# An MLP up-projection with seven block products in place of eight, in four token quarters, and score and value matmuls in alternating order

## The chip, the core and the metric

The kernel runs on one core of one Trainium2 chip. The core has a matrix engine (TensorE, PE in the profile, with PEld for its weight loads), a vector engine (VectorE, DVE), a scalar engine (ScalarE, ACT), a general engine (GpSimd, POOL) and a queue that issues transfers (SyncE, SP). Each engine takes its instructions in the order in which the program lists them. Matmul results go to PSUM, everything else lives in SBUF. The metric is the device time of one execution in microseconds.

## The reference

One inference step of a one-layer decoder: 2048 prompt tokens and 32 sample tokens (8 sequences of 4) of width 1024. Cut to what matters:

```python
p = einsum('btd,de->bte', h, w_in)                 # input projection
s = einsum('bnqgrd,bnkgd->bngrqk', qb, kk)         # scores of a 128-token window, head dim 64
o = einsum('bngrqk,bnkgd->bnqgrd', softmax(s), vv) # values
mixed = einsum('bte,ed->btd', concatenate([y_ssm, o], -1), w_out)
x = layer_norm(ALPHA * x + g_m * mixed)
h = x * (1.0 + sc_f) + sh_f
u = square(relu(einsum('btd,df->btf', h, w_up)))   # 1024 -> 4096
f = einsum('btf,fd->btd', u, w_down)               # 4096 -> 1024
x = layer_norm(ALPHA * x + g_f * f)
```

All inputs and outputs are float32. The kernel forms nearly every large product in three matmuls on rounded halves: each operand is split into a high part and a remainder (`hi` and `lo`), and `hi*hi + hi*lo + lo*hi` is accumulated in PSUM.

## The kernel before

The program has four stages: the first sweep over 17 token tiles (input projection of dt, q, k, v and the windowed attention), a second sweep (the state-space branch), the output projection with its LayerNorm, and the MLP. A scheduler that works on estimated durations lays out the order of each engine from the order of the calls, so an edit can move instructions that it doesn't touch.

In the first sweep `st_score` forms the scores of a tile with 24 matmuls `sc<-kTh,qh` (lines 166 to 168) whose contraction is 64 rows; four heads sit in rows 0 to 63 and four in rows 64 to 127 of the array, and the code issues all of one half's matmuls of a group before the other's. `st_PV` (line 462) issues the two 64-column halves of the value product in turn.

In the MLP the 2048 prompt tokens go in two halves of 1024. For each of 32 blocks of 128 hidden columns, `up` multiplies the block's weights (8 blocks of 128 rows) with the half's activations `H`, in groups of 512 columns (first half) or of 352 (second half, which takes the 32 sample tokens along): 8 x 3 matmuls a group. ScalarE takes relu and square, VectorE squares again in full precision (line 1269) and GpSimd forms the remainder (line 1270). `down` then takes two blocks at a time: 8 token tiles x 2 column halves x 2 blocks x 3 matmuls of 512 columns; VectorE adds each result from PSUM to an SBUF accumulator (line 1299). The weights come from HBM once a half. An up block is split by ScalarE (hi, line 162) and GpSimd (lo, line 163); a down block is first multiplied by the gate row `gf` on VectorE (line 1137). At the half's end the accumulators are normalised and stored (`finish`), and during each half the residual is added (lines 1230 to 1232).

## Time and profile before

| | us |
|---|---|
| three runs | 2469.86, 2470.47, 2472.53 (median 2470.47) |
| profiled execution | 2467.04, its span 2465.2 |
| MLP stage in the trace (first up matmul to last down matmul) | 978 to 2446 |
| output projection | 792 to 978 |
| first sweep's attention | 66 to 400 |

A row of the trace gives the start or the busy time, the engine, the line and the tiles `out<-in`. Busy times of one engine can't be added to another's, since the engines run side by side; an engine's busy time also holds the time in which an instruction has started and can't get on.

### The profile page before, as it was taken

How to read it: one execution, taken by the hardware profiler on the slowest of the kernel's cores; microseconds unless marked ns; L12 is line 12 of the kernel's file. 1: busy time of each engine (PE TensorE's matmuls, PEld its weight loads, DVE VectorE, ACT ScalarE, POOL GpSimd, SP SyncE). 2: the span in 40 equal slices, each digit the busy share in tenths (PEclk: the TensorE clock that was granted, in tenths of full speed). 3: DMA queues.
4: the chain of work that ended last, by engine and by line, in shares of the span. 5: the costliest groups of instructions: out<-in, count | busy, mean ns of one | idle time of the engine just before them, and what ended most of it. 6: DMA issues, size and time to landing. Idle time of an engine off the chain costs nothing.

```text
span 2465.2 us, 32266 instructions
## 1 busy us (share of the span) xinstructions
PE 2401.8 (97%) x12695; PEld 1997.0 (81%) x12695; DVE 1458.2 (59%) x2533; ACT 783.7 (32%) x1578; POOL 857.9 (35%) x587
## 2 busy tenths in 40 slices
PE   7899999999999999999999999999999999999997
PEld 6567777987897888887888888888889889889885
DVE  6756565987789776356555444448354554453448
ACT  3544455432333545421211212213412212212221
POOL 4333341233223222532332424327333333323335
PEclk9999999999999999999999999999999999999998
DMA  8754242223315346322121211118211211111111
GB/s 315 255 189 167 81 166 70 88 63 121 101 37 198 134 153 218 123 76 70 56 69 52 73 43 52 52 35 218 76 60 43 67 54 52 52 51 35 46 45 71
DMA packets 116104, 242.11 MB, mean 98 GB/s; under 512 B 26080, under 2 KB 61360, under 8 KB 112800
## 3 DMA queue, kind: packets, MB, share of 16 engines
q1 hardware_dynamic: 111552, 230.07, 27.9%
q10 hardware_dynamic: 4400, 9.98, 1.1%
q8 instruction: 100, 1.64, 0.3%
q14 instruction: 52, 0.43, 0.1%
HBM read 185.66 MB, written 55.37 MB: 98 GB/s over the span
## 4 chain that ended last, share of the span: by engine, by line
PE 49%; DVE 2%; POOL 1%; issue 1%; ACT 0%; DMA 0%; POOLq 0%; DVEq 0%; ACTq 0%
PE sc L166 10%; PE sc L168 10%; PE sc L167 10%; PE mm L166 5%; PE mm L168 5%; PE mm L167 5%; PE tr L166 1%; PE tr L168 1%; PE tr L167 1%; PE tr L1284 1%; DVE p L1299 1%; DVE nb L1311 0%; DVE p L1318 0%; POOL rs L174 0%; DVE bst L1332 0%
## 5 line engine op out<-in xcount | busy, mean ns | idle before, releaser
L163 POOL TENSOR_TENSOR wdl<-st,wdh 128x1024 fp32r<-128x1024 f32 x63 | 153.7, 2440 | 480.6 <-ACT wdh L162 480.6
L1269 DVE TENSOR_TENSOR r<-r 128x320 f32<-128x320 f32 (+1 forms) x160 | 131.1, 821 | 300.0 <-ACT A L1265 102.4
L1299 DVE TENSOR_TENSOR p<-mm,p 128x512 f32<-128x512 f32 x278 | 187.7, 685 | 123.2 <-PE mm L168 123.0
L162 ACT ACTIVATE wdh<-st 128x1024 fp32r<-128x1024 f32 x63 | 66.9, 1061 | 558.7 <-PE mm L168 173.0
L166 PE MATMUL sc<-H,wvh 128*128 128x352 f32 (+1 forms) x640 | 225.6, 352 | 5.0 <-ACT r L1263 5.0
L167 PE MATMUL sc<-H,wvh 128*128 128x352 f32 (+1 forms) x640 | 225.8, 353 | 0.0
L168 PE MATMUL sc<-H,wvl 128*128 128x352 f32 (+1 forms) x640 | 225.6, 352 | 0.0
L166 PE MATMUL sc<-H,wuh 128*128 128x352 f32 (+1 forms) x640 | 223.8, 350 | 0.0
L168 PE MATMUL sc<-H,wul 128*128 128x352 f32 (+1 forms) x640 | 223.1, 349 | 0.0
L167 PE MATMUL sc<-H,wuh 128*128 128x352 f32 (+1 forms) x640 | 222.9, 348 | 0.0
L1263 ACT ACTIVATE r<-sc 128x352 f32<-128x352 f32 (+1 forms) x160 | 81.6, 511 | 292.1 <-PE sc L168 281.9
L1137 DVE TENSOR_TENSOR st<-st,gf 128x1024 f32<-128x1024 f32 x64 | 112.6, 1759 | 95.4 <-POOL wdl L163 65.5
L166 PEld LDWEIGHTS sc<-H,wvh 128*128 128x128 f32 x640 | 120.6, 189 | 17.8 <-ACT r L1263 5.4
L167 PEld LDWEIGHTS sc<-H,wvh 128*128 128x128 f32 x640 | 120.6, 188 | 12.3
L168 PEld LDWEIGHTS sc<-H,wvl 128*128 128x128 f32 x640 | 120.5, 188 | 11.9
L166 PEld LDWEIGHTS sc<-H,wuh 128*128 128x128 f32 x640 | 120.1, 188 | 11.1 <-ACT r L1263 0.8
L168 PEld LDWEIGHTS sc<-H,wul 128*128 128x128 f32 x640 | 120.5, 188 | 10.2
L167 PEld LDWEIGHTS sc<-H,wuh 128*128 128x128 f32 x640 | 120.3, 188 | 10.0
L174 POOL TENSOR_TENSOR rs<-ve,mhalf 128x1 f32<-128x1 f32 (+2 forms) x68 | 48.5, 713 | 204.6 <-DVE ve L173 187.8
L653 DVE SCALAR_TENSOR_TENSOR xc<-xq,cvw,xc 128x256 f32<-128x256 f32 x192 | 102.2, 536 | 2.7
L1268 DVE TENSOR_TENSOR ud<-r 128x32 f32<-128x32 f32 x32 | 48.2, 1506 | 91.1 <-ACT r L1263 91.1
L163 POOL TENSOR_TENSOR wvl<-st,wvh 128x1024 fp32r<-128x1024 f32 x32 | 77.1, 2411 | 63.7 <-ACT wvh L162 60.7
(489 smaller groups left out, 6567.3 us busy)
## 6 DMA issues: line engine op xcount, KB each, us to landing
st<-in_wd SPq DMA_DIRECT2D x64, 512.0 KB
st<-in_wu SPq DMA_DIRECT2D x63, 512.0 KB
wa<-in_w_ada SPq DMA_DIRECT2D x32, 512.0 KB
hT_d<-hb SPq DMA_DIRECT2D x16, 1024.0 KB
hT<-hT_d SPq DMA_DIRECT2D x16, 512.0 KB
hT<-hT_d SPq DMA_DIRECT2D x8, 1024.0 KB
csb<-cs_d SPq DMA_DIRECT2D x16, 512.0 KB
st<-xhat_d SPq DMA_DIRECT2D x16, 512.0 KB
```

Of the source, the lines that this page charges most:

```text
L162: S.activation(hi, src, AF.Copy)
L163: (eng or V).tensor_tensor(lo, src, hi.bitcast(F32), ALU.subtract)
L166: PE.matmul(out, lhsT=ahi, rhs=bhi, start=first, stop=False)
L167: PE.matmul(out, lhsT=ahi, rhs=blo, start=False, stop=False)
L168: PE.matmul(out, lhsT=alo, rhs=bhi, start=False, stop=last)
L174: G.tensor_tensor(r[:P], v[:P], mhalf[:P, 0:n], ALU.pow)
L653: V.scalar_tensor_tensor(dst_, src(j), cvw[:, f, j:j + 1], dst_, ALU.mult, ALU.add)
L1137: V.tensor_tensor(st, raw, scale, ALU.mult)
L1263: S.activation(r[:, :n], mm[:, :n], AF.Relu)
L1268: V.tensor_tensor(ud, r[:, w:n], r[:, w:n], ALU.mult)
L1269: V.tensor_tensor(r[:, :w], r[:, :w], r[:, :w], ALU.mult)
L1299: V.tensor_tensor(acc[t][:, sl], mm, acc[t][:, sl], ALU.add)
```

## The change

Two edits. In the first sweep, the score matmuls of the two halves of the array are now issued in turn (rows 64 to 127, rows 0 to 63, and so on), tied into that order by `side_by_side`; each group of two heads gets a PSUM bank of its own, and the first is tied behind a projection matmul (`mid`). The value matmuls are tied in turn in the same way. On TensorE, one tile's scores, before and now (kTh, kTl, qh, ql: high and low parts of keys and queries; sc and mm are PSUM banks):

```order
L166 MATMUL sc<-kTh,qh 128x256
L167 MATMUL sc<-kTl,qh 128x256
L168 MATMUL sc<-kTh,ql 128x256
L166 MATMUL sc<-kTh,qh 128x256
L167 MATMUL sc<-kTl,qh 128x256
L168 MATMUL sc<-kTh,ql 128x256
```

```order
L440 MATMUL mm<-kTl,qh 128x256
L440 MATMUL sc<-kTl,qh 128x256
L440 MATMUL mm<-kTh,ql 128x256
L440 MATMUL sc<-kTh,ql 128x256
L440 MATMUL mm<-kTh,qh 128x256
L440 MATMUL sc<-kTh,qh 128x256
```

What moved: the three products of one head came one after another, and now the same product of two heads in different rows stands side by side.

In the MLP, the tokens go in four quarters of 512 (the last with the 32 sample tokens), and one step takes a pair of hidden blocks (256 columns). The product of a 2 x 2 block matrix of weights (hidden block by half of the 1024 rows) with a 2 x 2 block matrix of activations (half of the rows by even or odd token tile) is formed from seven products of sums of blocks instead of eight products. Each product has 4 x 3 matmuls of 256 columns (272 in the last quarter). The sums of activation blocks (`h_ops`) are formed once a quarter, those of weight blocks (`up_ops`) once for each pair in each quarter, and the results are put together from PSUM by seven VectorE additions and one ScalarE copy a step. Both weight matrices are now loaded, scaled and split four times instead of twice. ScalarE's relu and square become one VectorE instruction on each hidden block (line 1339).

One turn of VectorE's work in the MLP, before (one turn is two hidden blocks and 1024 tokens; r: relu; st<-st,gf: scaled down weights; p: accumulators; mm and tr: PSUM banks):

```order
L1137 TENSOR_TENSOR st_13033<-st,gf 128x1024
L1269 TENSOR_TENSOR r<-r 128x512
L1137 TENSOR_TENSOR st_13041<-st,gf 128x1024
L1269 TENSOR_TENSOR r<-r 128x512 x2
L1299 TENSOR_TENSOR p_10009<-tr,p_10009 128x512
L1269 TENSOR_TENSOR r<-r 128x512
L1299 TENSOR_TENSOR p_10009<-mm,p_10009 128x512
L1299 TENSOR_TENSOR p_10010<-mm,p_10010 128x512 x2
L1299 TENSOR_TENSOR p_10011<-tr,p_10011 128x512 x2
```

and the first part of one now (two hidden blocks and 512 tokens; ws, wra, wrc, w1l, wBl: sums of weight blocks and their remainders; U, c: sums of products, sc: the products in PSUM; ho holds the gate row):

```order
L1175 TENSOR_TENSOR ws<-wrc 128x512
L1177 TENSOR_TENSOR wrc<-wra,wrc 128x512
L1325 TENSOR_TENSOR U_14189<-sc,X_14188 128x256
L1255 TENSOR_TENSOR st_14549<-p_14545,ho 128x1024
L1325 TENSOR_TENSOR c_14191<-sc,X_14188 128x256
L1325 TENSOR_TENSOR c_14191<-sc,U_14189 128x256
L1172 TENSOR_TENSOR w1l<-ws,w1h 128x512
L1325 TENSOR_TENSOR U_14190<-sc,U_14189 128x256
L1178 TENSOR_TENSOR wra<-ws,wra 128x512
L1325 TENSOR_TENSOR c_14192<-sc,U_14190 128x256
L1374 TENSOR_TENSOR p_13898<-tr,p_13898 128x512
L1179 TENSOR_TENSOR wra<-wra 128x512
```

What moved: the additions that free PSUM stood in rows of their own, and now stand one by one between additions whose inputs are both in SBUF.

GpSimd's order, one step now (u and B: remainders of the hidden values; wCl, wAl: of weight sums; wdl: of down weights); before, the same four weight splits and four remainders served twice the tokens:

```order
L172 TENSOR_TENSOR wdl<-st_16521,wdh 128x1024
L1345 TENSOR_TENSOR B_16272<-c_16170,A_16271 128x512
L1172 TENSOR_TENSOR wCl<-wrc,wCh 128x1024
L1345 TENSOR_TENSOR B_16272<-c_16171,A_16271 128x512
L172 TENSOR_TENSOR wdl<-st_16529,wdh 128x1024
L1172 TENSOR_TENSOR wAl<-wra,wAh 128x1024
```

What moved: nothing stands between the four weight splits of a step but the two remainders.

The diff, cut to its core:

```diff
+    def side_by_side(calls, prev=None):
+        for fn in calls:
+            ins = fn()
+            if prev is not None:
+                tc.add_manual_dep(ins.ins, prev.ins.name,
+                                  mybir.DependencyInfo(mybir.DependencyClass.NoSync, mybir.DependencyReason.DATA),
+                                  reason="side_by_side")
+            prev = ins
...
+        mid = tl.pop("mid", None)
+        rp = lambda par: slice(64 * par, 64 * par + 64)
         for g in range(2):
+            scs = [(sc_tile, mm_tile)[g * par]().rearrange("p (j s n) -> p j s n", j=2, s=2) for par in range(2)]
+            side_by_side([lambda jj=jj, i=i, par=par: PE.matmul(
+                scs[par][:, jj, 0:nk, :], lhsT=(ql if i == 2 else qh)[rp(par), 2 * g + jj, :],
+                rhs=(kTl if i == 1 else kTh)[rp(par), g, slots, :], start=i == 0, stop=i == 2)
+                for jj in range(2) for i in range(3) for par in (1, 0)], mid)
             for par in range(2):
-                sc = sc_tile().rearrange("p (j s n) -> p j s n", j=2, s=2)
-                rp = slice(64 * par, 64 * par + 64)
-                for jj in range(2):
-                    q2 = 2 * g + jj
-                    mm3(sc[:, jj, 0:nk, :], qh[rp, q2, :], ql[rp, q2, :], kTh[rp, g, slots, :], kTl[rp, g, slots, :])
+                sc = scs[par]
...
-        for i, (vv, pt) in enumerate(terms):
-            for g in range(2):
-                PE.matmul(o[64 * g:64 * g + 64, :], lhsT=vv[:, 64 * g:64 * g + 64], rhs=pt[:, g, :],
-                          start=i == 0, stop=i == len(terms) - 1, tile_position=(0, 64 * g))
+        side_by_side([lambda i=i, vv=vv, pt=pt, g=g: PE.matmul(
+            o[64 * g:64 * g + 64, :], lhsT=vv[:, 64 * g:64 * g + 64], rhs=pt[:, g, :], start=i == 0,
+            stop=i == len(terms) - 1, tile_position=(0, 64 * g))
+            for i, (vv, pt) in enumerate(terms) for g in (1, 0)])
...
+    def h_ops(e, o, sl):
+        b11, b21, b12, b22 = e[:, 0:4], e[:, 4:8], o[:, 0:4], o[:, 4:8]
+
+        def put(i, t):
+            S.activation(HH[i][:, :, sl], t, AF.Copy)
+            (V if i % 2 else G).tensor_tensor(HL[i][:, :, sl], t, HH[i][:, :, sl].bitcast(F32), ALU.subtract)
+
+        put(0, b11)
+        V.tensor_tensor(b12, b12, b11, ALU.subtract)
+        put(1, b12)
+        put(5, b22)
+        V.tensor_tensor(b22, b22, b12, ALU.subtract)
+        put(2, b22)
+        V.tensor_tensor(b11, b22, b11, ALU.subtract)
+        put(3, b21)
+        V.tensor_tensor(b21, b21, b22, ALU.subtract)
+        put(4, b11)
+        put(6, b21)
...
+    def up_ops(p, s1, wa, w1, wb, wc):
+        ra, rc = wup[p]
+
+        def put(w, t, eng):
+            S.activation(w[0], t, AF.Copy)
+            eng.tensor_tensor(w[1], t, w[0].bitcast(F32), ALU.subtract)
+
+        put(wa, ra, G)
+        V.tensor_tensor(s1, rc[:, 0], rc[:, 1], ALU.add)
+        put(w1, s1, V)
+        V.tensor_tensor(rc[:, 0], ra[:, 0], rc[:, 0], ALU.subtract)
+        V.tensor_tensor(ra[:, 0], s1, ra[:, 0], ALU.subtract)
+        V.tensor_tensor(ra[:, 1], ra[:, 1], ra[:, 0], ALU.subtract)
+        put(wb, ra, V)
+        put(wc, rc, G)
+        half = lambda w, i: (w[0][:, i], w[1][:, i])
+        wup[p] = [half(wa, 0), w1, half(wb, 0), half(wa, 1), half(wc, 0), half(wb, 1), half(wc, 1)]
...
+    def w_up(p):
+        up_ld(p, *[w3(wt(1024, "wr" + c, 2 - i, F32), 2) for i, c in enumerate("ac")])
+
+    def w_sums(p):
+        two = lambda n: [wt(1024, n + c) for c in "hl"]
+        up_ops(p, wt(512, "ws", 1, F32), [w3(t, 2) for t in two("wA")], [wt(512, "w1" + c) for c in "hl"],
+               [w3(t, 2) for t in two("wB")], [w3(t, 2) for t in two("wC")])
+
+    def w_down(f, w=None):
+        st = prt(6 + f % 2)
+        D.dma_start(out=st, in_=I["wd"][f])
+        hi, lo = w or [wt(1024, "wd" + c, 3) for c in "hl"]
+        s2 = wt(1024, "st2", 1, F32)
+        V.tensor_tensor(s2, st, gf, ALU.mult)
+        split(hi, lo, s2, G)
+        return hi, lo, st
...
+    def residual(q):
+        a = []
+        bg.append([lambda: a.append(row_a(q, 2))])
+
+        def mul(j):
+            r = spare(q, 1)
+            D.dma_start(out=r, in_=xhat1_d[128 * tok(q, j):128 * tok(q, j) + 128])
+            V.tensor_tensor(r, r, a[0], ALU.mult)
+            V.tensor_tensor(acc[q, j], acc[q, j], r, ALU.add)
+
+        def add(j):
+            V.tensor_tensor(acc[q, j], acc[q, j], a[1], ALU.add)
+
+        for j in range(4):
+            bg.extend([[lambda j=j: mul(j)], [], []])
+        bg.append([lambda: a.append(row_a(q, 3))])
+        for j in range(4):
+            bg.extend([[lambda j=j: add(j)], []])
...
+    def h_load(q):
+        for i in range(2):
+            e, o = [spare(q - 1, k).rearrange("p (k n) -> p k n", k=8) for k in range(2)]
+            D.dma_start(out=e, in_=h2_d[4 * q + 2 * i])
+            D.dma_start(out=o, in_=h2_d[4 * q + 2 * i + 1])
+            h_ops(e, o, slice(128 * i, 128 * i + 128))
...
+    def up(p, q):
+        N = 272 if q == 3 else 256
+        w = wup.pop(p)
+        x1, u2, u3 = [wt(272, nm, 1, F32)[:, :N] for nm in ("X1", "U2", "U3")]
+        c = [p4.tile([128, 2, 272], F32, tag=f"c{i}", name=f"c{i}") for i in range(2)]
+        cb = lambda i, j: c[i][:, j, :N]
+
+        def prod(o):
+            r = sc_tile()[:, :N]
+            for k in range(4):
                 ks = slice(128 * k, 128 * k + 128)
-                mm3(mm[:, :n], wh[:, ks], wl[:, ks], H[j][0][:, k, :n], H[j][1][:, k, :n], k == 0, k == 7)
-            r = t4("r")
-            S.activation(r[:, :n], mm[:, :n], AF.Relu)
-            w = min(n, 1024 - o)
-            S.activation(uh[:, o:o + w], r[:, :w], AF.Square)
-            if w < n:
-                ud = p4.tile([128, 32], F32, tag="ud", name="ud", bufs=4)
-                V.tensor_tensor(ud, r[:, w:n], r[:, w:n], ALU.mult)
-            V.tensor_tensor(r[:, :w], r[:, :w], r[:, :w], ALU.mult)
-            G.tensor_tensor(ul[:, o:o + w], r[:, :w], uh[:, o:o + w].bitcast(F32), ALU.subtract)
-            slot()
+                mm3(r, w[o][0][:, ks], w[o][1][:, ks], HH[o][:, k, :N], HL[o][:, k, :N], k == 0, k == 3)
+            return r
+
+        add = lambda out, r, t: V.tensor_tensor(out, r, t, ALU.add)
+        S.activation(x1, prod(0), AF.Copy)
+        add(u2, prod(2), x1)
+        add(cb(0, 0), prod(3), x1)
+        p5 = prod(1)
+        add(cb(0, 1), p5, u2)
+        add(u3, prod(4), u2)
+        add(cb(1, 1), p5, u3)
+        slot()
+        add(cb(0, 1), prod(5), cb(0, 1))
+        add(cb(1, 0), prod(6), u3)
+        uh, ul = u_pair()
+        ud = []
+        for i in range(2):
+            V.scalar_tensor_tensor(c[i][:, :, :N], c[i][:, :, :N], 0.0, c[i][:, :, :N], ALU.max, ALU.mult)
+            h3_ = lambda t: t[:, i].rearrange("p (a n) -> p a n", a=2)
+            S.activation(h3_(uh), c[i][:, :, 0:256], AF.Copy)
+            if q == 3:
+                ud.append(p4.tile([128, 32], F32, tag="ud", name="ud", bufs=4))
+                V.tensor_copy(ud[i].rearrange("p (a n) -> p a n", a=2), c[i][:, :, 256:272])
+            G.tensor_tensor(h3_(ul), c[i][:, :, 0:256], h3_(uh).bitcast(F32), ALU.subtract)
+        slot()
         return uh, ul, ud
...
-        for j in range(8):
-            t = t0 + j
+                    r = 32 * (2 * (i % 2) + n)
+                    PE.matmul(dec[r:r + 32, :], lhsT=ul_[i][2], rhs=w[2][:, 512 * n:512 * n + 512],
+                              start=p == 0 and i < 2, stop=p + i // 2 == 15, tile_position=(0, r))
+        for j in range(4):
             o = 128 * j
+            if p == 0:
+                acc_open(q, j)
             for n in range(2):
                 sl = slice(512 * n, 512 * n + 512)
-                mm = mm_tile() if dnc[0] % 5 < 3 else tr_tile() if dec is None else sc_tile()
+                mm = mm_tile() if q == 3 or dnc[0] % 5 < 3 else tr_tile()
...
+    for q in range(4):
+        if q == 3:
             dec = tr_tile()
...
+        us, ws = {0: step(0, q)}, {0: [w_down(0), w_down(1)]}
+        for p in range(15):
+            us[p + 1] = step(p + 1, q)
+            if q == 3 and p == 14:
                 break
...
+            if p:
+                ws[p] = [w_down(2 * p), w_down(2 * p + 1)]
+            down(q, [us.pop(p)], ws.pop(p), p, dec)
+            if q == 0:
+                next(ds, None)
+            if p == 1:
+                bg.extend([] for _ in range(4))
+                residual(q)
+                if q == 3:
+                    bg.extend([[], [dec_res]])
+        if q == 3:
             break
...
+        ws[15] = [w_down(30), w_down(31)]
+        h_load(q + 1)
+        for i in range(10):
             todo = []
...
+            for lag, fn in ((1, lambda j, q=q: finish(q, j)), (3, lambda j, q=q: y_store(tok(q, j), acc[q, j], 128, S))):
+                if 0 <= i - lag < 8 and (i - lag) % 2 == 0:
+                    todo.append(lambda fn=fn, j=(i - lag) // 2: fn(j))
             bg.append(todo)
...
+        down(q, [us.pop(15)], ws.pop(15), 15, dec)
```

More of the change, by code (lines that the diff above doesn't have):

```diff
@@ L167, in mm3 @@
         PE.matmul(out, lhsT=ahi, rhs=blo, start=False, stop=False)
[L168 removed]
+        return PE.matmul(out, lhsT=alo, rhs=bhi, start=False, stop=last)
     def rstd_of(p, var, P, n=1, scale=1.0):
@@ L1131, in wtile @@
-    def wtile(nm, f, hi, lo, scale=None, eng=None, st=None):
-        if (nm, f) not in pre:
-            wraw(nm, f, st)
-        raw = st = pre.pop((nm, f))
-        if scale is not None:
-            st = t4("st2")
-            V.tensor_tensor(st, raw, scale, ALU.mult)
-        split(hi, lo, st, eng or G)
-        return hi, lo, raw
-    def wu_pq():
-        return [pq.tile([128, 1024], F32R, tag="wu" + c, name="wu" + c) for c in "hl"]
-    wu = {}
+                S.activation(ho[:, k, :], tr[:, kk, :], AF.Identity, bias=AB2[:, 1, k:k + 1], scale=AB2[:, 0, k:k + 1])
@@ L1164, in body @@
     ph = pool("h2", side="right")
-    H2 = [[ph.tile([128, 8, 512], F32R, name=f"H2_{j}{i}") for i in range(2)] for j in range(2)]
+    HH, HL = [[ph.tile([128, 4, 272], F32R, name=f"H{c}{o}") for o in range(7)] for c in "hl"]
     p3 = pool("out")
@@ L1191, in body @@
     p4 = pool("ffn")
-    T4 = {"st": (3, F32), "st2": (1, F32), "wvh": (1, F32R), "wvl": (1, F32R),
-          "r": (2, F32), "gf": (1, F32), "wdh": (3, F32R), "wdl": (3, F32R)}
-    def q4(tag):
-        nb, ty = T4[tag]
-        return p4.tile([128, 512 if tag == "r" else 1024], ty, tag=tag, name=tag, bufs=nb)
-    f4 = {tag: q4(tag) for tag in T4}
-    def t4(tag):
-        return f4.pop(tag) if tag in f4 else q4(tag)
-    gf = t4("gf")
-    fr = {nm: p4.tile([128, 1024], F32, tag=nm, name=nm) for nm in ("ag1", "ab1", "g2", "b2")}
+    gf = q2("ho")
@@ L1234, in residuals @@
-    def residuals(t0, gap, step):
-        for _ in range(gap):
-            bg.append([])
-        for j in range(8):
-            bg.append([lambda j=j: acc_res(t0 + j)])
-            for _ in range(step - 1):
-                bg.append([])
+        return [w3(q2(nm, F32R), 2) for nm in (("x1", "u1"), ("A2", "B2"))[ucnt[0] % 2]]
     bg = []
@@ new lines, in body, with acc_open, spare, row_a @@
+    tok = lambda q, j: 4 * q + (0, 2, 1, 3)[j]
+    def acc_open(q, j):
+        acc[q, j] = prt((4 * q + j) % 6)
+    def spare(q, i):
+        return prt((4 * q + 4 + i) % 6)
+    def row_a(q, j):
+        a = bcast(spare(q, 0), I["rows"][j])
+        S.activation(a, a, AF.Copy, scale=ALPHA)
+        return a
+    def residual(q):
[13 more added lines that the diff above has]
+            bg.extend([[lambda j=j: add(j)], []])
@@ L1272, in up, with down @@
         return uh, ul, ud
     dnc = [0]
-    def wdown(f):
-        return wtile("wd", f, t4("wdh"), t4("wdl"), gf)
-    def down(us, ws, f0, t0, dec, after=None):
+    def down(q, us, ws, p, dec, after=None):
+        ul_ = [(u[0][:, i], u[1][:, i], u[2][i] if u[2] else None) for u in us for i in range(2)]
         if dec is not None:
@@ L1390, in dec_steps @@
         yield
-        oh, ol = [p4.tile([128, 8, ND], F32R, name="dh%d" % i) for i in range(2)]
+        oh = p4.tile([128, 8, ND], F32, name="dh")
         tr = tr_tile().rearrange("p (k n) -> p k n", n=ND)
@@ L1394, in dec_steps @@
             PE.transpose(tr[:, k, :], a[:, 128 * k:128 * k + 128], ident[:ND, :ND])
-        split(oh, ol, tr[:, 0:8, :])
-        for i, t in enumerate((oh, ol)):
-            D.dma_start(out=h2_d[8][:, i, :, :ND], in_=t.bitcast(F32))
+        S.activation(oh, tr[:, 0:8, :], AF.Copy)
+        h_ops(oh[:, :, 0:16], oh[:, :, 16:32], slice(256, 272))
         yield
```

218 lines of the change are left out of this document (74 added, 144 removed).

## The prediction

> **What bounds the kernel now.** I read the page's busy times first, then the busy times by stage, then TensorE's waits, and only then single rows.
>
> ```profile
> PE 2401.8 (97%) x12695; PEld 1997.0 (81%) x12695; DVE 1458.2 (59%) x2533; ACT 783.7 (32%) x1578; POOL 857.9 (35%) x587
> ...
> core 0: us, PE busy (x) PEld busy (x) DVE busy (x) ACT busy (x) POOL busy (x), PEclk, DMA share, GB/s
> 66.00:400.00 334.00, 315.13 (x1869) 231.04 (x1869) 221.37 (x556) 176.50 (x533) 115.58 (x89) 0.96 0.44 155
> 978.00:1681.00 703.00, 702.39 (x3044) 568.82 (x3043) 338.55 (x381) 162.04 (x224) 250.40 (x131) 1.00 0.23 71
> 1681.00:2447.00 766.00, 761.04 (x4020) 669.71 (x4018) 392.86 (x498) 179.72 (x284) 288.04 (x187) 1.00 0.19 62
> ...
> 1681.00:1721.00 40.00, 35.04 (x186) 32.14 (x185) 37.06 (x55) 15.00 (x18) 31.52 (x18) 0.96 0.77 216
> ...
> PE sc L166 <- ACT r L1263: 5.0, 1, 5.0
> ```
>
> The two MLP halves (978 to 1681, 1681 to 2447) take 703 + 766 = 1469 us, and TensorE is busy in 1463 of them: it sets the end there. VectorE and GpSimd are busy about half and a third of that time. One short stretch differs: where the halves meet, VectorE is busy 37.06 and GpSimd 31.52 of 40 us, and there TensorE falls to 35.04, with one wait of 5.0 us. In the attention stage TensorE is busy 315 of 334 us.
>
> **TensorE's part of the change.** The pitch of matmuls is read from starts, first and last of a run without a break: up, 512 columns (15 matmuls); down, 512 (42); up, 352 (37); and 256 columns in the second sweep (12), a width that the MLP had not used.
>
> ```profile
> 1499.71 0.39 PE L166 MATMUL sc<-H,wuh 128*128 128x512 f32 x1
> ...
> 1502.89 0.39 PE L168 MATMUL sc<-H,wul 128*128 128x512 f32 x1
> 1503.12 0.40 PE L166 MATMUL mm<-wdh,u 128*128 128x512 f32 x1
> ...
> 1512.64 0.40 PE L168 MATMUL mm<-wdh,ho 128*128 128x512 f32 x1
> ...
> 1999.79 0.32 PE L168 MATMUL sc<-H,wvl 128*128 128x352 f32 x1
> ...
> 2005.55 0.32 PE L168 MATMUL sc<-H,wul 128*128 128x352 f32 x1
> ...
> 606.77 0.28 PE L166 MATMUL mm<-hT,Wx 128*128 128x256 f32 x1
> ...
> 608.07 0.28 PE L168 MATMUL mm<-hT,Wx 128*128 128x256 f32 x1
> ```
>
> That is 3.18/14 = 0.227, 9.52/41 = 0.232, 5.76/36 = 0.160 and 1.30/11 = 0.118 us. Up before: 32 blocks x 24 matmuls x (2 x 0.227 + 3 x 0.160) = 717 us. Up now: 16 pairs x 84 matmuls x (3 x 0.118 + 0.125) = 644 us, 0.125 being the line between 256 and 352 columns at 272. The eighth product gone is worth 12%, narrower matmuls give some of it back, and 73 us are left. Down keeps its 3072 matmuls. TensorE's step (one pair, one quarter) is 84 x 0.118 + 48 x 0.232 = 21.0 us, and TensorE alone would bring the MLP to 1469 - 73 = 1396 us.
>
> **What the other engines take on.** VectorE and GpSimd stand in each other's way, but only in some rows. Starts and durations, VectorE then GpSimd:
>
> ```profile
> 1507.16 0.68 DVE L1299 TENSOR_TENSOR p<-mm,p 128x512 f32<-128x512 f32 x1
> 1507.76 0.67 DVE L1299 TENSOR_TENSOR p<-tr,p 128x512 f32<-128x512 f32 x1
> ...
> 1528.49 1.23 DVE L1137 TENSOR_TENSOR st<-st,gf 128x1024 f32<-128x1024 f32 x1 [2.18 <-POOL wdl L163]
> ...
> 1533.83 1.21 DVE L1137 TENSOR_TENSOR st<-st,gf 128x1024 f32<-128x1024 f32 x1
> ...
> 1543.66 0.69 DVE L1269 TENSOR_TENSOR r<-r 128x512 f32<-128x512 f32 x1 [2.96 <-ACT A L1265]
> ...
> 1729.43 3.23 DVE L1230 TENSOR_TENSOR st<-st,ag 128x1024 f32<-128x1024 f32 x1 [1.22 <-DMA st<-xhat_d]
> ...
> 1738.71 2.21 DVE L1268 TENSOR_TENSOR ud<-r 128x32 f32<-128x32 f32 x1 [2.96 <-ACT r L1263]
> ...
> L892 DVE TENSOR_TENSOR h<-h,sc 128x256 f32<-128x256 f32 x16 | 6.7, 416 | 8.4 <-PE sc L889 8.1
> ...
> 1507.31 1.30 POOL L1270 TENSOR_TENSOR ulx<-r,x 128x512 fp32r<-128x512 f32 x1 [0.63 <-DVE r L1269]
> ...
> 1533.99 2.21 POOL L1270 TENSOR_TENSOR B<-r,u 128x512 fp32r<-128x512 f32 x1 [0.63 <-DVE r L1269]
> ...
> 1729.16 2.42 POOL L163 TENSOR_TENSOR wvl<-st,wvh 128x1024 fp32r<-128x1024 f32 x1
> ...
> 1738.46 2.41 POOL L163 TENSOR_TENSOR wul<-st,wuh 128x1024 fp32r<-128x1024 f32 x1 [1.68 <-PE tr L1284]
> ```
>
> An addition with one input in PSUM (L1299) runs in 0.67 us in the middle of GpSimd's instruction of 1507.31. A row with both inputs in SBUF does not: L1230 started at 1729.43, GpSimd's split ended at 1731.58, and L1230 ended 1.08 us later, which is its own clean time; even 32 columns (L1268) took 2.21 us. GpSimd waits likewise: 2.21 instead of 1.30 us behind the L1137 of 1533.83. So these rows exclude each other. [...]
>
> Now one step, with rows that follow each other starting 0.08 us before the end (1507.16 + 0.60). VectorE: 8 accumulations x 0.60, 7 additions of 256 columns from PSUM x 0.34, 7 rows of 512 with both inputs in SBUF x 0.61 (four weight sums, one remainder, two of line 1339), and 3 of 1024 x 1.15 (two gate products, one remainder): 4.8 + 2.4 + 4.3 + 3.4 = 14.9 us. GpSimd: four remainders of 1024 x 2.40 and two of 512 x 1.30 = 12.2 us. Before, the same splits and remainders served two quarters at once.
>
> The rows that exclude each other are 7.7 + 12.2 = 19.9 us of the 21.0, so all of GpSimd's time must fall into VectorE's PSUM rows (7.2 us) or its idle time. In the new order the 15 PSUM rows stand in eight runs between the others, 0.9 us each. A GpSimd instruction begins when a VectorE row lets go or its own input comes, and covers about one run before VectorE meets the next row of both inputs in SBUF and stands: 4 x 0.9 + 2 x 0.8 = 5.2 us covered, 7.0 us not. VectorE then needs 14.9 + 7.0 = **21.9 us a step**, more than TensorE. Bounds: 7.2 covered gives 19.9 (TensorE's 21.0 then decides), nothing covered 27.1. I take 21.9, since the stretch 1681 to 1721 shows what two engines so loaded do to TensorE. What is late next: the additions that empty the three product banks stand behind the waiting rows in VectorE's order, so TensorE waits at its fourth product; and L1178 overwrites a tile in place that GpSimd's `wAl` reads, so it waits for GpSimd by order too.
>
> Work that TensorE's time covered before, and that now adds to an engine that is full: the residual, 12 rows of 1.15 a quarter, 14 x 4 = 55 us; and at each of three quarter ends VectorE's 8 statistics x 0.60, 4 products x 1.15 and 14 rows of `h_ops` x 0.61, 18 us, with 4 x 2.40 + 8 x 1.30 = 20 us on GpSimd, uncovered at the same 7.0 of 12.2: 11 us. 3 x 29 = 88 us.
>
> MLP: 64 x 21.9 + 55 + 88 = 1545 us against 1469: **+76 us**.
>
> ScalarE's share costs nothing: five splits of 1024 or 512 and three small copies a step are below 8 us by the row here, against 21.9. Nor do the transfers: four of 512 KB a step are 2.1 MB in 21.9 us, 96 GB/s, which by 0.19 at 62 GB/s is a share of 0.3. If GpSimd's delay holds a weight buffer back, its next load lands late in the row at the head of VectorE's order (`ws`); that is part of the second rival.
>
> ```profile
> L162 ACT ACTIVATE wdh<-st 128x1024 fp32r<-128x1024 f32 x63 | 66.9, 1061 | 558.7 <-PE mm L168 173.0
> ...
> 202.17 0.28 PE L167 MATMUL sc<-kTl,qh 64*128 64x256 f32 x2
> 202.29 0.28 PE L168 MATMUL sc<-kTh,ql 64*128 64x256 f32 x2
> ...
> 208.81 0.28 PE L167 MATMUL sc<-kTl,qh 64*128 64x256 f32 x1
> 208.93 0.28 PE L168 MATMUL sc<-kTh,ql 64*128 64x256 f32 x1
> ...
> 210.49 1.08 PE L462 MATMUL sc<-PT,v 128*64 128x512 f32 x4
> ```
>
> **Attention.** Scores start every 0.12 us, one alone (208.81) or two at once where the order happens to bring different rows together (202.17). In the tile shown 12 of 24 go in pairs; pairing the rest saves 6 x 0.12 = 0.7 us a tile, 11 us in 15 tiles. The values run four in 1.08 us, in pairs already; I take 2 us for tiles where they are broken up. 13 us off, since TensorE is nearly full there. Bounds: 22 us for 360 score matmuls all alone before and another 10 for values; the other way, up to 10 us lost if the tied order makes TensorE wait for the softmax.
>
> **Sum.** 2467 + 76 - 13 = 2530 us for an execution like the profiled one, which lies 3 below the median shown: **2533 us**. Its own range, with 21.3 to 22.8 us a step, is 2490 to 2595.
>
> **Rivals.**
> 1. TensorE stays the bound. For it: 19.9 is below 21.0, and the order puts PSUM additions between the others. Against it: that leaves 1.1 us a step, and the residual alone needs 14 us a quarter. MLP 1396 us, plus at three quarter ends the activation sums' 29 us, less the two last down turns that cover them (2 x 11), 7 us each: 1417. 2467 - 52 - 13 + 3 = **2405 us**. It decides if more than 6.1 us of a step's GpSimd time is covered. [...]
> 2. GpSimd covers half as much (2.6 us), because its instructions follow each other without letting VectorE in, and the weight buffers come free late: 24.5 us a step, 64 x 24.5 + 55 + 3 x 34 = 1725, +256: **2713 us**.
> 3. Both meet, or the sums' cost just eats the 73 us: within 0.2% (5 us, about what a measurement here can tell from no change).
>
> **Chances.** Forecast 0.48, rival 1 0.34, rival 2 0.13, rival 3 0.05. So faster 0.34, same 0.05, slower 0.61. The range reaches into rival 1 (its own bounds of the attention, 2390 to 2425) and into the lower part of rival 2: 2392 to 2640.
>
> **What would show it.** Right: MLP about 1545 us with TensorE busy well below it, its waits ended by VectorE's `U` and `c` additions; rows of lines 1175 to 1179 and 1255 far above 0.69 and 1.23 us in the mean; VectorE busy over 90%. Wrong: TensorE busy throughout, or MLP below 1430 us (rival 1); waits for GpSimd's remainders or for weight loads in front (rival 2). An attention stage that is not shorter than 334 us refutes that term.

## The result, and the profile after

The changed kernel takes 2654.9 us (2651.1 to 2660.4) against 2470.2 us (2468.0 to 2472.5): 1.0749 of the time before, 95% interval 1.0724 to 1.0775. The forecast was 2533 us, its range 2392 to 2640. The direction was right; the time lies above the range.

The page's busy times of the changed kernel, then busy times by stretch (the attention stage, the second sweep with the output stage, and the four quarters of the MLP, cut where each quarter's first up product starts), then what VectorE, TensorE and the transfer queue wait for between 966 and 2644 us (total, times, longest):

```profile
PE 2396.3 (90%) x14231; PEld 2015.6 (76%) x14231; DVE 2250.1 (85%) x3465; ACT 958.7 (36%) x1751; POOL 1275.9 (48%) x705
```

```profile
66.00:370.00 304.00, 274.10 (x1725) 203.48 (x1717) 199.03 (x504) 153.55 (x495) 116.05 (x89) 0.94 0.48 169
370.00:967.00 597.00, 588.13 (x3564) 506.76 (x3565) 463.36 (x1037) 245.51 (x508) 147.36 (x126) 1.00 0.35 120
967.00:1374.00 407.00, 359.88 (x2106) 308.91 (x2104) 375.42 (x430) 133.37 (x181) 233.77 (x106) 0.97 0.32 108
1374.00:1789.00 415.00, 362.98 (x2113) 314.89 (x2112) 387.85 (x443) 134.18 (x173) 247.66 (x113) 0.95 0.30 99
1789.00:2207.00 418.00, 363.57 (x2112) 314.91 (x2111) 386.00 (x443) 134.37 (x173) 248.63 (x113) 0.95 0.29 99
2207.00:2644.00 437.00, 396.60 (x2264) 327.69 (x2262) 385.70 (x478) 132.96 (x164) 246.99 (x113) 0.97 0.24 83
```

```profile
DVE ws L1175 <- DMA wrc<-in_wu: 48.1, 34, 4.2
DVE w1l L1172 <- ACT w1h L1171: 24.5, 25, 1.0
...
PE sc L175 <- DVE U L1325: 100.0, 63, 5.1
PE sc L175 <- DVE c L1325: 42.6, 22, 7.9
...
SPq L1164 <- POOL wCl L1172: 120.0, 40, 8.3
```

The MLP grew from 1468 to 1677 us, by 209, and began 12 us earlier. VectorE, which was idle half of it before, is now busy 375 to 388 us of each quarter's 407 to 437, and TensorE, which was idle for 6 us in all, waits for VectorE's `U` and `c` additions. VectorE itself waits too: 48 us for the load of `wrc`, 25 us for ScalarE's `w1h`.

The groups of VectorE in the MLP (busy us, mean ns of one, then idle time before them) show what its rows cost beside their clean 680 and 1210 ns:

```profile
L1255 DVE TENSOR_TENSOR st<-p,ho 128x1024 f32<-128x1024 f32 x128 | 218.3, 1705 | 15.0 <-DMA p<-in_wd 10.4 <-POOL wdl L172 4.6
L1374 DVE TENSOR_TENSOR p<-mm,p 128x512 f32<-128x512 f32 x326 | 216.2, 677 | 5.8 <-PE mm L177 5.8
...
L1172 DVE TENSOR_TENSOR wBl<-wra,wBh 128x1024 fp32r<-128x1024 f32 x63 | 121.2, 1923 | 3.0 <-ACT wBh L1171 3.0
L1172 DVE TENSOR_TENSOR w1l<-ws,w1h 128x512 fp32r<-128x512 f32 x63 | 114.0, 1810 | 25.5 <-ACT w1h L1171 24.5
L1175 DVE TENSOR_TENSOR ws<-wrc 128x512 f32<-128x512 f32 x63 | 96.9, 1538 | 48.1 <-DMA wrc<-in_wu 48.1
...
L1344 DVE COPY ud<-c 128x32 f32<-128x32 f32 x32 | 26.3, 821 | 0.1
...
L1407 DVE BATCH_NORM_STATS2 bst<-p 128x6 f32<-128x512 f32 x24 | 15.5, 676 | 0.0
```

The accumulations with an input in PSUM (L1374) keep their 677 ns; rows with both inputs in SBUF take up to 2.7 times their own. From all of VectorE's rows I made an account of the MLP. A row's own time is the shortest of its form (the third percentile), less 0.08 us where the next row starts before its end; what it took beyond that is "blocked" (the account doesn't tell what blocks a row; that it is GpSimd, the runs below show); time between rows is "idle". The forecast's terms sort into the same columns: 64 x 14.9 + 55 + 3 x 18 own, 64 x 7.0 + 3 x 11 blocked.

| VectorE in the MLP, us | own | blocked | idle | stage |
|---|---|---|---|---|
| before | 575 | 156 | 733 | 1468 |
| forecast | 1063 | 481 | 0 | 1545 |
| changed | 1058 | 474 | 139 | 1677 |

Own and blocked came out within 7 us of the forecast, and the miss of 132 us stands in the idle column (the three columns add up to the stage to about 1%, here and in the runs below). By rows, the agreement of the blocked column is partly luck: about 370 us of it stand at the rows of the steps, where 448 were forecast, and about 100 at the residual, the decode copies and the quarter ends, where 33 were.

One step shows all three. It is one of the regular ones: between the starts of every 84th up matmul, the last six pairs before a quarter's final one take 23.2 us in the mean (first three quarters). The first nine pairs take 25.3 to 26.4 in the mean, since the residual and what is left of the quarter end before fall among them. The rows are starts and durations of VectorE, then GpSimd, then ScalarE, of the changed kernel from one `ws` row to the next:

```profile
1661.47 1.86 DVE L1175 TENSOR_TENSOR ws<-wrc 128x512 f32<-128x512 f32 x1 [1.30 <-DMA wrc<-in_wu]
1663.25 0.68 DVE L1374 TENSOR_TENSOR p<-mm,p 128x512 f32<-128x512 f32 x1
...
1665.38 2.50 DVE L1255 TENSOR_TENSOR st<-p,ho 128x1024 f32<-128x1024 f32 x1
1667.80 0.41 DVE L1325 TENSOR_TENSOR c<-sc,X 128x256 f32<-128x256 f32 x1
1668.14 0.41 DVE L1325 TENSOR_TENSOR c<-sc,U 128x256 f32<-128x256 f32 x1
1669.53 2.47 DVE L1172 TENSOR_TENSOR w1l<-ws,w1h 128x512 fp32r<-128x512 f32 x1 [0.98 <-ACT w1h L1171]
...
1676.46 2.31 DVE L1172 TENSOR_TENSOR wBl<-wra,wBh 128x1024 fp32r<-128x1024 f32 x1
...
1680.22 1.38 DVE L1339 SCALAR_TENSOR_TENSOR c<-c 128x512 f32<-128x512 f32 x1
...
1684.47 2.08 DVE L1175 TENSOR_TENSOR ws<-wrc 128x512 f32<-128x512 f32 x1 [1.07 <-DMA wrc<-in_wu]
```

```profile
1664.39 2.40 POOL L1172 TENSOR_TENSOR wAl<-wra,wAh 128x1024 fp32r<-128x1024 f32 x1 [1.61 <-ACT wAh L1171]
1669.05 2.40 POOL L172 TENSOR_TENSOR wdl<-st,wdh 128x1024 fp32r<-128x1024 f32 x1 [2.25 <-ACT wdh L171]
...
1677.64 3.41 POOL L1172 TENSOR_TENSOR wCl<-wrc,wCh 128x1024 fp32r<-128x1024 f32 x1
```

```profile
1667.91 1.06 ACT L171 ACTIVATE wdh<-st 128x1024 fp32r<-128x1024 f32 x1 [3.60 <-DVE st L1255]
1668.88 0.62 ACT L1171 ACTIVATE w1h<-ws 128x512 fp32r<-128x512 f32 x1
```

From 1661.47 to 1684.47 are 23.0 us. Five rows are blocked, by 1.18 + 1.29 + 1.79 + 1.10 + 0.70 = 6.1 us. Two waits make 0.98 + 1.07 = 2.05 us. The other 14.9 us are the rows' own. The `w1l` row shows a chain: `st` is blocked by GpSimd's `wAl` until 1666.79 and ends at 1667.88, so ScalarE makes `wdh` late and `w1h` behind it; VectorE idles 0.98 us for `w1h`; in that gap GpSimd takes `wdl`, and VectorE then stands 1.79 us more. The `ws` row shows another: GpSimd's `wCl` is itself blocked (3.41 in place of 2.40 us) and ends at 1681.05; only then is the one `wrc` buffer free, its load lands 3.4 us later, and VectorE, with nothing else that its order allows, waits for it.

### The profile page after: what moved, and what is told of

Same layout as the page of the kernel before. It is cut to its first block, busy times and chain, and to the rows that moved or that the text cites. A ratio compares the mean times of both kernels' runs of the same rounds, so it can differ in the third digit from the quotient of the medians.

```text
span 2658.6 us, 37118 instructions
## 1 busy us (share of the span) xinstructions
PE 2396.3 (90%) x14231; PEld 2015.6 (76%) x14231; DVE 2250.1 (85%) x3465; ACT 958.7 (36%) x1751; POOL 1275.9 (48%) x705
## 5 line engine op out<-in xcount | busy, mean ns | idle before, releaser
L172 POOL TENSOR_TENSOR wdl<-st,wdh 128x1024 fp32r<-128x1024 f32 x127 | 331.2, 2608 | 208.9 <-ACT wdh L171 197.0
L175 PE MATMUL sc<-Hh,wCh 128*128 128x256 f32 (+1 forms) x504 | 158.3, 314 | 127.2 <-DVE U L1325 98.0
L1172 POOL TENSOR_TENSOR wCl<-wrc,wCh 128x1024 fp32r<-128x1024 f32 x63 | 184.5, 2929 | 105.7 <-ACT wCh L1171 97.9
L1255 DVE TENSOR_TENSOR st<-p,ho 128x1024 f32<-128x1024 f32 x128 | 218.3, 1705 | 15.0 <-DMA p<-in_wd 10.4
L1374 DVE TENSOR_TENSOR p<-mm,p 128x512 f32<-128x512 f32 x328 | 217.5, 677 | 5.8 <-PE mm L177 5.8
L1172 POOL TENSOR_TENSOR wAl<-wra,wAh 128x1024 fp32r<-128x1024 f32 x63 | 166.8, 2648 | 65.5 <-ACT wAh L1171 65.5
L175 PE MATMUL sc<-Hh,wBh 128*128 128x256 f32 (+1 forms) x504 | 149.1, 296 | 16.9 <-DVE c L1325 11.3
L175 PE MATMUL mm<-wdh,A 128*128 128x512 f32 x358 | 145.7, 410 | 14.9 <-DVE p L1374 14.7
L1339 DVE SCALAR_TENSOR_TENSOR c<-c 128x512 f32<-128x512 f32 (+1 forms) x128 | 152.0, 1187 | 0.3
L177 PE MATMUL sc<-Hh,wCl 128*128 128x256 f32 (+1 forms) x504 | 150.5, 299 | 0.0
L176 PE MATMUL sc<-Hl,wCh 128*128 128x256 f32 (+1 forms) x504 | 150.4, 298 | 0.0
```

What stands on the lines that cost most here:

```text
L172: (eng or V).tensor_tensor(lo, src, hi.bitcast(F32), ALU.subtract)
L175: PE.matmul(out, lhsT=ahi, rhs=bhi, start=first, stop=False)
L176: PE.matmul(out, lhsT=ahi, rhs=blo, start=False, stop=False)
L177: return PE.matmul(out, lhsT=alo, rhs=bhi, start=False, stop=last)
L1172: eng.tensor_tensor(w[1], t, w[0].bitcast(F32), ALU.subtract)
L1255: V.tensor_tensor(s2, st, gf, ALU.mult)
```

## The experiments

Times are medians; the kernel before ran beside them at 2468.3 to 2469.9 us. "Account" is VectorE's own / blocked / idle time in the MLP, worked out as above.

### Attention alone

The kernel before with the changed kernel's score and value loops:

```diff
+            side_by_side([lambda jj=jj, i=i, par=par: PE.matmul(scs[par][:, jj, 0:nk, :], ...)
+                for jj in range(2) for i in range(3) for par in (1, 0)], mid)
-                    mm3(sc[:, jj, 0:nk, :], qh[rp, q2, :], ql[rp, q2, :], kTh[rp, g, slots, :], kTl[rp, g, slots, :])
```

> The kernel before with only the alternating score and value matmuls. The prediction's term: 13 us off, 2457 us (its bounds 31 off to 10 on). In the changed kernel the MLP began 12 us earlier, which says the same; if that was luck of the order in the longer program, this run stands within 5 us of 2470. The score stage should end about 30 us earlier than the kernel before's 392 us and give part of that back in the sweep behind it.

Measured: 2452.3 us (2451.5 to 2455.0), 0.9935 of the kernel before (0.9922 to 0.9947), 16 us off. By the starts of the matmuls the last score ends at 358.6 instead of 392.5 us, and the MLP begins at 961.3 instead of 978.4: half of the 34 us is given back. This run's busy times from 66 us on, up to 366 and up to the MLP, say why:

```profile
66.00:366.00 300.00, 271.79 (x1731) 201.56 (x1730) 199.78 (x504) 153.56 (x496) 116.32 (x89) 0.96 0.50 172
366.00:961.00 595.00, 586.82 (x3557) 505.77 (x3557) 463.88 (x1016) 247.89 (x504) 167.49 (x132) 1.00 0.35 118
```

and the kernel before from 400 us to the MLP:

```profile
400.00:978.00 578.00, 570.40 (x3400) 488.71 (x3400) 449.99 (x964) 239.93 (x479) 167.12 (x132) 0.99 0.36 121
```

The kernel before had 1869 matmuls in the 334 us up to 400; here 1731 stand in the 300 up to 366. Part of the shortening is work that the order moved into the next sweep, which has 3557 where it had 3400. The term of 13 us was right in what it is worth at the end, and the trace bears out its mechanism: of the 384 score matmuls, 87 pairs start within 0.03 us of each other in the kernel before and 185 here, and 98 pairs more at 0.12 us are 12 us, where the prediction had 11 for the scores.

### GpSimd's remainders on VectorE

```diff
-        put(wa, ra, G)
+        put(wa, ra, V)
-        put(wc, rc, G)
+        put(wc, rc, V)
-        split(hi, lo, s2, G)
+        split(hi, lo, s2, V)
```

> The changed kernel with the remainders of wA, wC and of the two down weights on VectorE (1.15 us each there) in place of GpSimd (2.40 us each). Theory (rows with two SBUF inputs and GpSimd exclude each other): VectorE's own work rises by 256 x 1.15 = 294 us, from 1058 to 1352 us, but GpSimd keeps only 831 - 601 = 230 us, of which at most 132 us (the share now uncovered) are waited for; VectorE needs 1352 + 132 + its idle 139 = 1623 us at most and 1490 us if the rest is covered, so the kernel gets faster though its fullest engine gets more to do: 2470 to 2603 us, 2550 most likely. Rival (VectorE is full of its own rows, and their length has nothing to do with GpSimd): 294 us slower, 2950 us.

Measured: 2510.6 us (2507.8 to 2513.5), 144 us less than the changed kernel. Account 1342 / 147 / 48: VectorE has 284 us more to do, is 327 us less blocked and 91 us less idle. The rival's 2950 us is out. This run separates a full engine from an engine that is kept waiting: the same work cost less on the fuller engine. By the account the exchange of blocked for own time is worth only 43 us of the 144; most of the gain is in VectorE's own waits (139 us before, 48 here), which went with GpSimd's long rows.

```profile
L1255 DVE TENSOR_TENSOR st<-p,ho 128x1024 f32<-128x1024 f32 x128 | 171.8, 1342 | 4.9 <-DMA p<-in_wd 4.0 <-DMA ho<-ada_d 0.8
...
L1172 DVE TENSOR_TENSOR wBl<-wra,wBh 128x1024 fp32r<-128x1024 f32 x63 | 83.1, 1318 | 0.3 <-ACT wBh L1171 0.2
```

The gate product (L1255) falls from 1705 to 1342 ns, `wBl` from 1923 to 1318, with nothing changed in them. The wait for `wrc`, 48 us before, is 6.6 us here, although `wrc` still has one buffer: in the changed kernel it was late mostly because of GpSimd.

### GpSimd's weight remainders left out

```diff
-            eng.tensor_tensor(w[1], t, w[0].bitcast(F32), ALU.subtract)
+            if eng is not G:
+                eng.tensor_tensor(w[1], t, w[0].bitcast(F32), ALU.subtract)
...
+        wa, wc = (wa[0], wa[0]), (wc[0], wc[0])
```

> The changed kernel without GpSimd's weight remainders: wA, wC and the down weights enter the matmuls with their rounded part in the remainder's place, so the matmuls stay as many and as wide, and GpSimd loses 601 us of work. Theory: VectorE's own work stays 1058 us, what GpSimd blocks of it falls from 474 to 130 us at most, so VectorE has 1190 us to do in a time that TensorE sets: MLP 1396 to 1470 us, the kernel 2380 to 2450 us. Rival (VectorE's own rows or the late weight loads bind by themselves, whatever GpSimd does): no more than the loads' 48 us faster, 2600 to 2655 us.

Measured: 2412.7 us (2409.3 to 2417.9). Account 1089 / 105 / 246. The time is in the theory's range. With GpSimd nearly empty the MLP is TensorE's, as in the first rival, and what that rival needed is seen: not that more of GpSimd's time is covered, but that there is little of it (287 us busy instead of 977). VectorE, which has time to spare here, still waits 30 us for `wrc`, so GpSimd was not the only reason that this load comes late.

```profile
965.00:2395.00 1430.00, 1406.04 (x8595) 1236.83 (x8593) 1181.57 (x1791) 545.12 (x689) 287.23 (x187) 0.99 0.34 113
```

### A second buffer for `wrc`

```diff
-        up_ld(p, *[w3(wt(1024, "wr" + c, 2 - i, F32), 2) for i, c in enumerate("ac")])
+        up_ld(p, *[w3(wt(1024, "wr" + c, 2, F32), 2) for i, c in enumerate("ac")])
```

> The changed kernel with two buffers instead of one for the second half of the up weights (wrc), room for which comes from two tiles of the stage before. VectorE waits 48 us in the MLP for this load. Theory: that wait adds to the blocked time, and the kernel gets faster by about it, 2607 us (2590 to 2625). Rival: GpSimd works on in these waits and VectorE meets it later instead, so that the time stays within 10 us of 2655.

Measured: 2625.2 us (2624.2 to 2627.3), 30 us off and not 48. Account 1071 / 435 / 145. The wait for `wrc` is gone, and a regular step takes 21.7 us instead of 23.2, but VectorE's idle time is as long as before; it now waits at other rows:

```profile
DVE U L1326 <- PE sc L177: 35.3, 47, 5.4
DVE st L1256 <- POOL wdl L172: 35.0, 28, 2.7
```

The last pair of a quarter takes 44 to 47 us, where it took 40. So the single buffer was a real cost, but taking away the longest wait did not shorten the idle time: over five regular steps it stays at 2.2 to 2.3 us a step, while blocked time falls from 6.4 to 4.7. That the regular step now lies near the forecast's 21.9 is therefore luck. The time is at the upper bound of the first theory, whose mechanism (the wait simply drops out) was not what happened.

### Halves

```diff
-        split(hi, lo, s2, G)
+        S.activation(hi, s2, AF.Copy)
+        for h in range(2):
+            hs = slice(512 * h, 512 * h + 512)
+            G.tensor_tensor(lo[:, hs], s2[:, hs], hi[:, hs].bitcast(F32), ALU.subtract)
```

and the same for `wA` and `wC`.

> The changed kernel with GpSimd's weight remainders (wA, wC, down) each in two instructions of 512 columns in place of one of 1024. GpSimd's time a step rises from 12.2 to 10 x 1.30 = 13.0 us. Theory (each GpSimd instruction is covered by about one run of VectorE's PSUM rows, 0.9 us; ten instructions instead of six reach nearly all of the 7.2 us of such rows): blocked 5.8 us a step instead of 7.4, 2555 to 2600 us. Rival (GpSimd's instructions follow each other without letting VectorE in, so what is blocked goes with GpSimd's time): 474 x 13.0/12.2 = 505 us, 2685 us.

Measured: 2576.6 us (2573.2 to 2578.3), 78 us off. Account 1065 / 414 / 130. GpSimd does the same work in more instructions, and the kernel gets faster: VectorE comes in between the halves. A pair of halves takes 3.40 us from start to end, not 2 x 1.30:

```profile
1629.93 3.40 POOL L1262 TENSOR_TENSOR wdl<-st,wdh 128x512 fp32r<-128x512 f32 x2
```

What is blocked fell by 0.9 us a step, not by the 1.6 that the theory asked for; the rest of the 78 us I can't assign. The time is inside the theory's range, the mechanism's size is not fully shown.

### The decode copies on ScalarE

```diff
-                V.tensor_copy(ud[i].rearrange("p (a n) -> p a n", a=2), c[i][:, :, 256:272])
+                S.activation(ud[i].rearrange("p (a n) -> p a n", a=2), c[i][:, :, 256:272], AF.Copy)
```

> The changed kernel with the 32 copies of the decode columns (line 1344, 128x32) on ScalarE in place of VectorE. They take 26.3 us on VectorE, 3 us by their own length. Theory (even this short copy is blocked by GpSimd, and the wait is lost): 20 to 30 us faster, 2630 us. Rival (VectorE then meets the same GpSimd instruction one row later, at the next row with two SBUF inputs): 2645 to 2655 us.

Measured: 2648.4 us (2645.0 to 2649.6), 6 us off, as the rival had it. Copies that looked like 26 us were worth 6. Account 1062 / 461 / 149: 13 us less blocked, 10 us more idle. With these rows gone VectorE met GpSimd at others: from 2207 to 2640 us L1255 went from 57.0 to 60.8 us, L1339 from 41.9 to 44.1 and L1177 from 9.5 to 11.7. What the blocked column holds can't be priced row by row.

### Residual and quarter ends

The residual left out:

```diff
-                residual(q)
+                bg.extend([] for _ in range(22))
```

> The changed kernel without the residual of the second normalisation for the prompt's tokens: its 48 rows of 1024 (lines 1292, 1293, 1296), their loads and the scaled gain rows are left out. The prediction's term is 55 us (own time alone): 2600 us. With the 30 us for which the profile of the changed kernel shows these rows blocked, and the 10 us that they wait for loads: 95 us, 2560 us. If VectorE were not the bound there: no change.

Measured: 2604.2 us (2601.8 to 2608.6), 51 us off. That is near the prediction's 55 and not the 95 that adds the blocked and idle time at these rows, the same lesson as with the copies.

The quarter ends left out:

```diff
-        h_load(q + 1)
...
-            for lag, fn in ((1, lambda j, q=q: finish(q, j)), (3, lambda j, q=q: y_store(tok(q, j), acc[q, j], 128, S))):
+            for lag, fn in ((3, lambda j, q=q: y_store(tok(q, j), acc[q, j], 128, S)),):
```

> The changed kernel without what stands at the three inner quarter ends: the last normalisation of these quarters (statistics, gain and shift) and the new activation sums are left out; the sums of the first quarter serve all four, and the rows are stored as they are. The prediction's term is 88 us: 2567 us. By the step times of the changed kernel's trace the last pair of a quarter takes 40.1 us in place of 23.2, 51 us in all, and the rows of the normalisation in the next quarter's first steps come on top: 2560 to 2600 us. If the two down turns at the end covered this work: above 2640 us.

Measured: 2569.5 us (2567.8 to 2569.9), 85 us off, against the prediction's 88. The regular step stayed at 23.2 us, and the last pair of a quarter fell from 40.1 to the same 23.2.

### Can the seven products win?

Two steps on the way. The square on ScalarE (on top of the remainders on VectorE):

```diff
-            V.scalar_tensor_tensor(c[i][:, :, :N], c[i][:, :, :N], 0.0, c[i][:, :, :N], ALU.max, ALU.mult)
+            S.activation(c[i][:, :, :N], c[i][:, :, :N], AF.Relu)
...
+            S.activation(c[i][:, :, :N], c[i][:, :, :N], AF.Square)
```

> The kernel with the weight remainders on VectorE (2511 us), and besides the maximum and the square of line 1339 on ScalarE (one maximum and two squares there, in place of VectorE's row and ScalarE's copy). VectorE's MLP account there was 1342 us of its own work, 147 blocked, 48 idle. Theory: its own work falls by 128 x 0.61 = 78 us to 1264; with 100 to 130 blocked and 48 idle that is 1410 to 1440 us, close to TensorE's 1396, and the MLP gets 1420 to 1455 us: 2400 to 2440 us, 2430 most likely. Rival (the longer chain on ScalarE, two rows more before the down matmuls, makes TensorE wait as long): no better than 2490 us.

and the last step remainder on VectorE too:

```diff
-            G.tensor_tensor(h3_(ul), c[i][:, :, 0:256], h3_(uh).bitcast(F32), ALU.subtract)
+            V.tensor_tensor(h3_(ul), c[i][:, :, 0:256], h3_(uh).bitcast(F32), ALU.subtract)
```

> As the run with the square on ScalarE, and the last remainders of the steps (ul, line 1345) on VectorE too, so that GpSimd has only the quarter ends' work. VectorE's own work 1264 + 128 x 0.61 = 1342 us, blocked 30 to 50 us by the quarter ends, idle 48. Theory: 1420 to 1440 us, TensorE and VectorE level, 2400 to 2430 us, and not slower than with ul on GpSimd. Rival (own rows are what counts once GpSimd is small; 2.6 us of GpSimd a step were covered anyway): 20 to 78 us slower than with ul on GpSimd.

Measured: 2492.3 us (2491.2 to 2493.3) and 2483.6 us (2480.7 to 2484.5). Both theories missed, by 52 and 54 us beyond their ranges, and the first time is what the square's rival allowed. Of the second, one part held: with the last remainders on VectorE too the kernel is 9 us faster, where the rival had it 20 to 78 us slower. The accounts, 1272 / 131 / 118 and 1347 / 61 / 108, have the own and the blocked time about as forecast, but 118 and 108 us idle where I had carried over the 48 of the run before: it is again the third column. The accounts don't show where in time it lies. Three stretches of the second kernel, the middle one around the first quarter end:

```profile
965.00:1325.00 360.00, 341.22 (x2102) 301.66 (x2102) 335.82 (x490) 166.80 (x242) 8.15 (x9) 1.00 0.37 120
1325.00:1370.00 45.00, 30.14 (x152) 27.16 (x152) 44.28 (x62) 19.33 (x27) 17.84 (x12) 0.73 0.32 112
1370.00:1695.00 325.00, 320.41 (x1967) 284.11 (x1965) 309.76 (x448) 151.86 (x211) 10.48 (x5) 1.00 0.35 113
```

Away from the end TensorE nearly sets the pace, busy in 341 of 360 and 320 of 325 us, with 21.2 us a step in the last ones; at the end VectorE is full (44.28 of 45) and TensorE gets 30.14 us, at a clock of 0.73. VectorE's spare time in the middle of a quarter can't be used at its end. I had compared two totals of the whole stage, which is the mistake of reading one average over the whole span, one level down. The square's rival had the time but hardly the cause: the longest of TensorE's waits in that run end on VectorE's `U` (18.5 us), and ScalarE's largest, 10.6 us, is for the activation sums of the quarter ends.

So VectorE needed to lose work that the quarters repeat. The first quarter now writes the weight sums and gated down weights to DRAM, and the other three load them:

```diff
+        if not pre:
+            S.dma_start(out=us_d[p][:, 0], in_=s1)
+            S.dma_start(out=us_d[p][:, 1:3], in_=ra)
+            S.dma_start(out=us_d[p][:, 3:5], in_=rc)
...
+        if q:
+            D.dma_start(out=s2, in_=gd_d[f])
+        else:
+            V.tensor_tensor(s2, st, gf, ALU.mult)
```

> A candidate: the kernel without GpSimd's step remainders (2484 us), and besides the first quarter writes its weight sums (w1, wB, wC) and its gated down weights to DRAM, and the other three read them in place of forming them again; wrc has two buffers. Theory: VectorE's own work loses 48 steps x (4 sums x 0.60 + 2 products x 1.15 = 4.7 us) = 226 us, from 1347 to 1121 us; the run without weight remainders, with 1089 us, spent 354, 353 and 383 us in the quarters 2 to 4, and the first quarter stays as it was, 367 us: MLP 1457 us, the kernel 2425 to 2455 us, 2440 most likely, below the kernel before. Rival (the transfers bind: 2.2 MB a pair written in the first quarter, 2.9 to 3.9 MB read a pair later in place of 2.1): no better than 2483 us.

Measured: 2425.9 us (2423.1 to 2427.3), 0.9818 of the kernel before (0.9804 to 0.9833): faster than both kernels, and than the kernel before with the attention edit alone (2452 us). Account 1142 / 57 / 252. By quarter:

```profile
964.00:1324.00 360.00, 347.52 (x2129) 305.98 (x2127) 337.65 (x502) 172.20 (x248) 12.15 (x10) 0.99 0.68 231
1324.00:1670.00 346.00, 337.46 (x2084) 301.94 (x2083) 278.70 (x397) 171.28 (x235) 28.27 (x16) 0.98 0.48 153
1670.00:2017.00 347.00, 341.45 (x2112) 305.05 (x2112) 283.78 (x411) 173.88 (x237) 26.38 (x16) 1.00 0.48 155
2017.00:2406.00 389.00, 384.30 (x2272) 322.54 (x2272) 287.24 (x451) 172.68 (x229) 29.71 (x18) 1.00 0.49 164
```

TensorE is busy in 1411 of 1442 us again; of the 73 us that the eighth product was forecast to be worth on TensorE, 26 arrive in the length of the MLP. The first quarter, which still forms the sums and moves 231 GB/s with what it writes, takes 360 us where the next two take 346 and 347.

## Why the prediction was wrong, point by point

- **TensorE's part** was right. Where TensorE sets the pace (the last steps of a quarter in the later runs), a step takes 21.2 us (forecast 21.0), and its 1396 us stand against 1406 busy in the run without weight remainders.
- **That VectorE and GpSimd exclude each other** was right. With GpSimd's weight remainders moved to VectorE or left out, rows that nobody had touched became shorter (`wBl` from 1923 to 1318 and 1315 ns), and the kernel by 144 and 242 us. Blocked time was forecast at 481 us and measured at 474, in the regular step 7.0 and 6.1 us; the share of GpSimd's own time that comes back as blocked time, 0.57 forecast, is 474 of 831 us. The sum is partly luck, as said above, and the working behind the share, one run of PSUM rows covered by each GpSimd instruction, is not shown: with ten instructions a step it asked for 1.6 us less and got 0.9.
- **The step that failed** is "VectorE then needs 14.9 + 7.0 = 21.9 us a step, more than TensorE". The sum of what an engine does, and of what blocks it, was taken for the length of the step; VectorE's own waits were set to nothing. The regular step measured 23.0 to 23.2 us, with 2.05 us of such waits, and VectorE's idle time in the MLP was 139 us, against a miss of 132. Less the residual and the quarter ends, at what leaving them out gained (51 and 85 us), the 1677 us are 24.1 us for each of the 64 pairs, against the 21.9. By quarters the stage was forecast at 393, 393, 393 and 364 us and took 407, 415, 418 and 436; idle are 29, 27, 32 and 51 us of that. In the last quarter VectorE's own work, 270 us against 252, adds 18 us: I had not counted the wider products' extra columns, the decode tokens' rows and the last statistics there. More than half of the miss, 72 us, is this last quarter, where VectorE waits mostly for TensorE's products (about 23 us) and for loads (17, of which `wrc` is 3).
- **"Nor do the transfers"** cost, was the same error. Their mean share of 0.3 was as worked out (0.24 to 0.32), but the load of `wrc`, which could only start when a blocked GpSimd row had freed its single buffer, was late at that share (48 us of waits). The prediction named this and left it to the second rival. The second buffer gained 30 us, though the idle time did not fall with it. What the rest of the idle time is made of is read from the waits (25 us for `w1h`, about 32 for TensorE's products, 24 for other loads), and not shown by a run; an order that makes `w1h` in time was not tried. So that VectorE's waits were left out of the step is shown, and what each wait costs stays open.
- **The residual** (55 forecast, 51 measured), **the quarter ends** (88 and 85) and **the attention** (13 and 16) were right to within 4 us. The condition set for the attention, a stage below 334 us, was met, but half of its gain was given back in the sweep behind it.
- **The rivals.** TensorE as the bound is what remains when GpSimd's work is gone, but not with it there. The second rival had the late buffers right and the covered time wrong: GpSimd covered as much as forecast, not half of it. Its 24.5 us a step lie above the regular 23.2, but near the 24.1 in the mean, and its 2713 us is 58 us off where the forecast is 122 off. The sign named for it, weight loads in front, came too: `ws` for `wrc` heads VectorE's waits.
- **The signs.** Rows of lines 1175 and 1255 (1538 and 1705 ns), VectorE's share (1535 of 1677 us, 92%), and TensorE's waits for `U` and `c` came as named. Lines 1177 to 1179 came in part: 1183, 945 and 803 ns in the mean, but their clean 680 in regular steps. The wait of L1178 for `wAl` by order, named as late next, came once, for 1.4 us. The 1545 us did not come.

## What to carry to other kernels

The length of a step is the sum of three parts on the fullest engine: its own rows, what blocks them, and what they wait for (here 14.9, 6.1 and 2.05 us); a forecast that leaves out the third is a lower bound, and a single buffer that is released by a blocked row is where to look for it (a second one gained 30 us here). Where two engines exclude each other, compare the time that an operation holds the other engine, not the time it takes: here a remainder of 1.15 us on the full VectorE was cheaper than 2.40 us on an idle GpSimd, a little by the account's blocked time (327 us for 284) and more by the waits that went with it (91 us). And compare sums stage by stage, down to the seams between repeated passes: VectorE's spare time inside a quarter (24 of 360 us) bought nothing at its end (44.28 of 45 us busy).
